# A two-layer decoder trunk on one core: input combinations of the up-projection taken off GpSimd, the last up-projection bank copied ahead of the SiLU, and a down-projection in eight groups

## The chip, the cores and the metric

The kernel runs on one core of a Trainium2 chip. The engines are named as in the profile: PE is TensorE's matrix unit (PEld its weight loads), DVE is VectorE, ACT is ScalarE, POOL is GpSimd, and SP is SyncE, which here only issues DMAs. Each engine works through its own list of instructions in order; an instruction that waits holds up everything behind it on that engine. The metric is the device time of one execution, in microseconds (us), as the median of several runs.

## The reference

Two layers; each has a token mixer (convolution, differential attention, spatial gating) and a channel mixer. Each of the two is wrapped in the same way, `x <- LayerNorm(alpha * x + (1 + gate) * f(x * (1 + scale) + shift))`. The change lies in the channel mixer:

```python
D_MODEL, SEQ, DEPTH = 1024, 1024, 2
FFN_DIM = ((8 * D_MODEL // 3 + 127) // 128) * 128      # 2816: 22 blocks of 128
FFN_KERNEL = 3

def conv_ffn(h, w_up, b_up, conv_w, conv_b, w_down, b_down):
    up = causal_dwconv(h @ w_up + b_up, conv_w, conv_b)
    g, val = jnp.split(up, 2, axis=-1)
    return (jax.nn.silu(g) * val) @ w_down + b_down
```

All data is fp32, batch 1. A product of two fp32 matrices is made of three matmuls on rounded parts: each operand is split into a high part (a cast, on ACT) and the remainder (a subtraction, on DVE or POOL), and high by high, low by high and high by low are added up (`mm3`, lines 128 to 132). Making those two parts is called a split below.

## The kernel before

A layer runs through these stages, with the times of layer 0 and layer 1 in the profiled execution: the mixer until 507 and 1732 us; the last group of its output projection with the LayerNorm of its rows (the boundary) until 530 and 1755; the transposes that turn the rows into inputs of the up-projection until 552 and 1776; the up-projection until 992 and 2206; the down-projection, and in layer 0 the LayerNorm and transposes into layer 1, until 1293 and 2483.

**Input combinations.** The up-projection is done with seven products of half size instead of eight (Strassen's scheme). Its right operands are four quarters of the transposed, modulated input and sums of them, here called B11, B21, B22, T1, T2, T3 and T4. `comb_early` runs once the first half of the rows is normalised, `comb_late` after the second. `comb_in` (L954) transposes four row tiles on PE and writes scale and shift with ACT (L958). `comb_split` (L960) is the split: a cast on ACT (L961) and a subtraction (L962) on the engine that it is given. Before, B22, T3 and T4 were split on POOL, the other four on DVE; the sums were on DVE (L974, L985) and POOL (L988, L989). The left operands (weights) have the same scheme; `up_first` (L1049) makes those of block 0 ahead of time, with four sums on POOL (L1055 to L1064) during the attention. One of its parts, the seventh weight a22, is split at the start of `up_phase` into a page of the tag Rb; it is only read by the last product of block 0, but its cast stands ahead of the copies of `up_phase` on ACT.

**Up-projection.** `up_phase` (L1078) goes over 22 blocks f; PE's, ACT's and DVE's order in it is written by hand (other instructions are put between these by the scheduler). A block is seven products (`product`) of 12 matmuls each, in the order 2, 5, 6, 3, 7, 1 of the next block, 4; products 3 and 1 of block 0 come first. Banks of PSUM are read by copies on ACT. Of the two halves of a block, the gate half `cg` is convolved (`taps`, two L1111 on DVE) and goes through the SiLU (L1193, ACT); the value half is copied from bank `pb` to `cv` (L1133, ACT) in the next turn of the loop, and so is the product of both and its DMA to d_act. For the last block this next turn does no products: it is only the copy, `lin`, `taps`, the multiplication and the DMA.

**Down-projection.** `ffn` (L1226) goes over the 22 blocks in groups of the sizes in L1244. For each block of a group it loads the activation (`load_act`, L1212) and the weight (`load_wdown`, L1218) and splits both. `out_group` (L874) then goes over eight row tiles: the products of the group add up in a pair of banks `og`, and DVE adds the pair to the running sum r (L887); the first group is copied by ACT instead (L885). Two sets of pages hold split operands in turn. After each group, `pump` takes so many steps of a background list: in layer 0 the 47 steps of the modulation of layer 1 (DVE multiply-adds L258 and L260 on DMAs of `wada`) and eight steps of the residual (`residual_in`, L1006: three 128x1024 DVE operations per row tile, L1016 to L1018, on `xr`, with `agab` and `xr` in pages of tag O+"b"); in layer 1 only the residual. The order of the list is fixed in the program, but a scheduler places the instructions on the engines by priority, so the work of later code may come ahead of that of earlier code.

**Boundary of the layers.** After the last group of layer 0, each row tile is normalised (`ln_rows`, L348 to L363; the reciprocal root is on POOL, L138), transposed (L333, PE) and split into the input of layer 1: ACT writes the scaled tile (L340) and its high part (L343), DVE the remainder (L346). Then PE starts the projection `prj` of layer 1.

## Time and profile before

| | us |
|---|---|
| runs, median (lowest to highest) | 2482.52 (2481.01 to 2484.5) |
| profiled execution | 2485.14 |
| its span, first to last instruction | 2483.4 |
| PE busy in it | 2323.6 (94%) |
| DVE busy | 1988.7 (80%) |
| ACT busy | 1049.6 (42%) |
| POOL busy | 402.4 (16%) |
| mean granted TensorE clock | 0.968 |

A row of the timeline reads: start, duration, engine, line, operation, output <- inputs, sizes, how many instructions are drawn together, and in brackets how long the engine was idle before it and which engine's instruction released it. A row of the windows reads: the stretch and its length, then for each engine the busy time and the number of instructions in it, the granted clock, the share of the DMA engines, and GB/s. A row of the waits reads: who waited for whom, us in total, times, longest. A 128x512 matmul at the full clock is drawn 0.39 us long but starts 0.227 us after the one before it.

### The profile page before, as it was taken

The page shows a single profiled execution, that of the slowest core. Times are in us where ns is not written, and L with a number is a line of the kernel's source. Part 1 is how long each engine was busy: PE and PEld are TensorE (multiplying, and loading weights), DVE is VectorE, ACT ScalarE, POOL GpSimd, SP SyncE. Part 2 cuts the span into 40 slices and gives each one's busy share as a digit, 9 for nine tenths or more (in the row PEclk, how much of TensorE's full clock was granted, in tenths as well). Part 3 has the DMA queues.
Part 4 walks back from the last instruction along what each step waited for, and adds up shares of the span by engine and source line. Part 5 has one row for each costly group of instructions (what it writes and reads, how often), then busy time and mean ns, then how long its engine had stood idle before and what let it go on. Part 6 is the DMA issues. An engine that isn't in the chain of part 4 may idle for free.

```text
span 2483.4 us, 28299 instructions
## 1 busy us (share of the span) xinstructions
PE 2323.6 (94%) x10846; PEld 1889.5 (76%) x10846; DVE 1988.7 (80%) x2618; ACT 1049.6 (42%) x1692; POOL 402.4 (16%) x213
## 2 busy tenths in 40 slices
PE   7998999979999999999689999999799999979996
PEld 7786777767888887788578877777588888868885
DVE  7898876788887888778979987657987777787768
ACT  4214754645554554311131157454555545542111
POOL 1144260441000000000020542123500000000003
PEclk9998899989999999999899998999899999989998
DMA  8433352122332334645523254220232222263311
GB/s 295 148 120 130 134 202 103 60 93 94 110 111 94 111 110 157 214 146 176 177 60 115 77 169 160 95 102 26 94 102 77 83 87 86 77 204 127 102 43 68
DMA packets 87673, 294.07 MB, mean 118 GB/s; under 512 B 9265, under 2 KB 18801, under 8 KB 86001
## 3 DMA queue, kind: packets, MB, share of 16 engines
q1 hardware_dynamic: 87536, 292.26, 35.1%
q8 instruction: 85, 1.39, 0.2%
q14 instruction: 52, 0.42, 0.1%
HBM read 228.23 MB, written 64.00 MB: 118 GB/s over the span
## 4 chain that ended last, share of the span: by engine, by line
PE 37%; DVE 9%; issue 3%; ACT 3%; POOL 2%; DMA 1%; SPq 0%; POOLq 0%; DVEq 0%; ACTq 0%
PE og L130 3%; PE og L131 3%; PE og L132 3%; PE upb L1074 3%; PE upb L1076 3%; PE upb L1075 3%; PE sc L733 2%; PE upd L1076 1%; PE upd L1074 1%; PE upd L1075 1%; PE pv L778 1%; DVE r L887 1%; PE of L130 1%; DVE dn L126 1%; PE of L132 1%
## 5 line engine op out<-in xcount | busy, mean ns | idle before, releaser
L130 PE MATMUL og<-dn,dn 128*128 128x512 f32 x704 | 280.3, 398 | 38.6 <-DVE r L887 22.0
L1074 PE MATMUL upb<-comb,uw 128*128 128x512 f32 x704 | 275.6, 392 | 8.6 <-DVE upc L1098 6.7
L1075 PE MATMUL upb<-comb,uw 128*128 128x512 f32 x704 | 275.3, 391 | 2.5 <-DVE comb L962 2.5
L131 PE MATMUL og<-dn,dn 128*128 128x512 f32 x704 | 277.6, 394 | 0.0
L132 PE MATMUL og<-dn,dn 128*128 128x512 f32 x704 | 277.2, 394 | 0.0
L1076 PE MATMUL upb<-comb,uw 128*128 128x512 f32 x704 | 274.9, 391 | 0.0
L138 POOL TENSOR_TENSOR lnrs<-lnrs,mhalf 128x1 f32<-128x1 f32 x32 | 21.2, 666 | 1398.7 <-DVE lnrs L137 1394.1
L1098 DVE TENSOR_TENSOR uw<-wu,uw 128x512 fp32r<-128x512 f32 x210 | 144.0, 686 | 125.2 <-ACT uw L1101 125.2
L1111 DVE SCALAR_TENSOR_TENSOR cv<-upc,pc,cv 128x1023 f32<-128x1023 f32 (+1 forms) x176 | 225.3, 1280 | 2.8
L887 DVE TENSOR_TENSOR r<-og,r 128x1024 f32<-128x1024 f32 x144 | 174.3, 1218 | 64.7 <-PE og L132 63.8
L130 PEld LDWEIGHTS og<-dn,dn 128*128 128x128 f32 x704 | 133.8, 190 | 73.8 <-DVE r L887 27.0
L410 DVE SCALAR_TENSOR_TENSOR convacc<-convy,pc,convacc 128x1023 f32<-128x1023 f32 (+14 forms) x120 | 176.2, 1469 | 2.3
L125 ACT CAST dn<-actr 128x1024 fp32r<-128x1024 f32 x44 | 46.0, 1050 | 310.4 <-PE og L131 146.4
L1074 PEld LDWEIGHTS upb<-comb,uw 128*128 128x128 f32 x704 | 132.7, 188 | 38.5 <-DVE upc L1098 8.4
L1075 PEld LDWEIGHTS upb<-comb,uw 128*128 128x128 f32 x704 | 132.7, 189 | 31.8 <-DVE comb L962 4.2
L1101 ACT CAST uw<-wu 128x512 fp32r<-128x512 f32 x210 | 121.6, 615 | 83.5 <-DVE wu L1098 77.0
L132 PEld LDWEIGHTS og<-dn,dn 128*128 128x128 f32 x704 | 133.8, 190 | 28.2
L131 PEld LDWEIGHTS og<-dn,dn 128*128 128x128 f32 x704 | 134.1, 190 | 26.8
L1076 PEld LDWEIGHTS upb<-comb,uw 128*128 128x128 f32 x704 | 132.7, 189 | 27.5
L1075 PE MATMUL upd<-comb,uw 128*128 128x512 f32 x352 | 138.2, 393 | 3.0 <-DVE comb L962 2.9
L1074 PE MATMUL upd<-comb,uw 128*128 128x512 f32 x352 | 138.0, 392 | 0.0
L1076 PE MATMUL upd<-comb,uw 128*128 128x512 f32 x352 | 137.3, 390 | 0.0
(315 smaller groups left out, 5554.4 us busy)
## 6 DMA issues: line engine op xcount, KB each, us to landing
wada<-in_w_ada SPq DMA_DIRECT2D x96, 512.0 KB, 4.5
wu<-in_w_up_t SPq DMA_DIRECT2D x84, 512.0 KB, 3.6
d_act<-cv SPq DMA_DIRECT2D x44, 512.0 KB, 2.6
actr<-d_act SPq DMA_DIRECT2D x44, 512.0 KB, 4.4
wdn<-in_w_down SPq DMA_DIRECT2D x44, 512.0 KB, 4.5
win<-in_w_fm SPq DMA_DIRECT2D x24, 512.0 KB, 4.2
wtm<-in_w_tm SPq DMA_DIRECT2D x16, 512.0 KB, 3.7
wout<-in_w_out SPq DMA_DIRECT2D x16, 512.0 KB, 6.0
```

What stands on the lines that cost most here:

```text
L130: mm(ps, lh, rh, start=first, stop=False)
L131: mm(ps, lh, rl, start=False, stop=False)
L132: mm(ps, ll, rh, start=False, stop=last)
L410: nc.vector.scalar_tensor_tensor(out=acc[:, d:], in0=y[:, :S - d], scalar=w(30 - d), in1=acc[:, d:], op0=ALU.mult, op1=ALU.add)
L733: nc.tensor.matmul(ps[m][:, c0:c1], q[ms, isl], k[ms, c0:c1], start=n == 0, stop=n == 2 and c1 != w)
L887: nc.vector.tensor_tensor(out=r[t], in0=ps, in1=r[t], op=ALU.add)
L1074: mm(ps, w[:, 0, ks], hi[k], start=k == 0 and not more, stop=False, skip_group_check=True)
L1075: mm(ps, w[:, 0, ks], lo[k], start=False, stop=False, skip_group_check=True)
L1076: mm(ps, w[:, 1, ks], hi[k], start=False, stop=k == 3, skip_group_check=True)
L1098: v.tensor_tensor(out=o, in0=x, in1=y, op=op)
L1101: act.copy(self.up_w[n][:, 0], src)
L1111: v.scalar_tensor_tensor(out=u[:, d:], in0=c[:, :S - d], scalar=self.ffw[:, 2 - d, m:m + 1], in1=u[:, d:], op0=ALU.mult, op1=ALU.add)
```

## The change

Three things are changed in both layers.

1. `comb_early`, `comb_late` and `up_first` issue nothing on POOL any more: all splits and sums of the inputs, and the four sums of the first weights, are on DVE. `comb_early` keeps only the transposes; the splits are put into `comb_late` in the order B22, B11, B21, T1, T2, T3, T4, and the sums are formed in other pages.
2. After the last product of the last block, `up_phase` copies its bank to `cv` at once, ahead of the SiLU in the list of ACT, and the next turn of the loop leaves the copy out.
3. The down-projection has eight groups (2, 3, 3, 3, 3, 3, 2, 3) instead of nine (2, 3, 3, 3, 3, 2, 2, 1, 3). The activations of the first group get two pages of tag O+"b" of their own, and the two sets of pages change places. `pump` takes 3n steps after a group of n instead of 3n + 2, and after the first group none in layer 1.

```diff
     def comb_early(self, r, H, sc, sh):
         nc = self.nc
         H["f3"] = self.parts("tmp", 2, F32)
-        f22 = self.parts("tmp", 2, F32)
+        H["f22"] = self.parts("tmp", 2, F32)
         for k in range(4):
-            self.comb_in(r, 1, k + 4, sc, sh, f22[k])
-            self.comb_split(H["B22"], k, f22[k], nc.gpsimd)
+            self.comb_in(r, 1, k + 4, sc, sh, H["f22"][k])
         for k in range(4):
-            f12, f3 = H["f12"][k], H["f3"][k]
-            self.comb_in(r, 1, k, sc, sh, f12)
-            nc.vector.tensor_tensor(out=f3, in0=f22[k], in1=f12, op=ALU.subtract)
-            self.comb_split(H["T3"], k, f3, nc.gpsimd)
+            self.comb_in(r, 1, k, sc, sh, H["f12"][k])
...
         f = self.parts("Rb", 2, F32) + self.parts("Rb", 2, F32)
-        f1, f2 = H["f12"], H["f3"]
-        for q in range(8):
+        f1, f2, f22 = H["f12"], H["f3"], H["f22"]
+
+        def tt(o, x, y, op):
+            nc.vector.tensor_tensor(out=o, in0=x, in1=y, op=op)
+        for k in range(4):
+            self.comb_split(H["B22"], k, f22[k], nc.vector)
+        for q in range(4):
             self.comb_in(r, 0, q, sc, sh, f[q])
-            self.comb_split(H["B11" if q < 4 else "B21"], q % 4, f[q], nc.vector)
+        for q in range(4):
+            self.comb_split(H["B11"], q, f[q], nc.vector)
+        for q in range(4, 8):
+            self.comb_in(r, 0, q, sc, sh, f[q])
+        for q in range(4, 8):
+            self.comb_split(H["B21"], q - 4, f[q], nc.vector)
         for k in range(4):
-            nc.vector.tensor_tensor(out=f1[k], in0=f1[k], in1=f[k], op=ALU.subtract)
+            tt(f2[k], f22[k], f1[k], ALU.subtract)
+            tt(f1[k], f1[k], f[k], ALU.subtract)
             self.comb_split(H["T1"], k, f1[k], nc.vector)
         for k in range(4):
-            nc.gpsimd.tensor_tensor(out=f2[k], in0=f2[k], in1=f[k], op=ALU.add)
-            nc.gpsimd.tensor_tensor(out=f[4 + k], in0=f[4 + k], in1=f2[k], op=ALU.subtract)
-            self.comb_split(H["T2"], k, f2[k], nc.vector)
+            tt(f[k], f2[k], f[k], ALU.add)
+            tt(f[4 + k], f[4 + k], f[k], ALU.subtract)
+            self.comb_split(H["T2"], k, f[k], nc.vector)
         for k in range(4):
-            self.comb_split(H["T4"], k, f[4 + k], nc.gpsimd)
+            self.comb_split(H["T3"], k, f2[k], nc.vector)
+        for k in range(4):
+            self.comb_split(H["T4"], k, f[4 + k], nc.vector)
...
-        tt = nc.gpsimd.tensor_tensor
+        tt = nc.vector.tensor_tensor
...
             if f:
-                act.copy(cv[:, 0:512], pb)
+                if run:
+                    act.copy(cv[:, 0:512], pb)
...
             pb = b
+            if not nxt:
+                act.copy(cv[:, 0:512], pb)
...
         yb, yc = pages(A + "b", 4), pages(A + "c", 4)
-        sets = [(ya[:6], yc + ya[6:]), (xa[:6], xa[6:] + yb)]
+        xb = []
+        for _ in range(2):
+            t = self.page(O + "b", "dn", F32R, (P, 2, 1024))
+            xb += [t[:, i] for i in range(2)]
+        sets = [(xa[:6], xa[6:] + yb), (ya[:6], yc + ya[6:])]
...
-        sizes = (2, 3, 3, 3, 3, 2, 2, 1, 3)
+        sizes = (2, 3, 3, 3, 3, 3, 2, 3)
...
-            acts, wts = (ya[:4], xc) if j == 0 else sets[j % 2]
+            acts, wts = (xb, xc) if j == 0 else sets[j % 2]
...
-                self.pump(2)
+                    self.pump(2)
...
-                self.pump(3 * n + 2 if l + 1 < L else 2)
+                self.pump(3 * n if l + 1 < L else 2)
```

Lines behind the change have other numbers in the changed kernel: L974, L985, L988 and L989 become L979, L1098 becomes L1107, L1133 becomes L1143 (and the new copy L1200), L1193 becomes L1205.

How the lists of instructions change is shown at three places. The first is DVE's list of layer 0 at the end of the combinations, before. `comb` are the combinations and their parts, `uw_849_4593` is the low part of weight a22, made from a page of `wuv` by its split, and `wus` and L1098 are the first sums of block 1.

```order
L962 TENSOR_TENSOR comb_758_4174<-comb_820_4460,comb_756_4172 128x512 x2
L126 TENSOR_TENSOR uw_849_4593<-wuv_740_4138,uw_849_4593 128x512
L962 TENSOR_TENSOR comb_759_4175<-comb_821_4461,comb_757_4173 128x512 x2
L962 TENSOR_TENSOR comb_750_4166<-comb_764_4180,comb_760_4176 128x512 x2
L962 TENSOR_TENSOR comb_750_4166<-comb_765_4181,comb_761_4177 128x512 x2
L962 TENSOR_TENSOR comb_751_4167<-comb_790_4290,comb_762_4178 128x512 x2
L962 TENSOR_TENSOR comb_751_4167<-comb_791_4291,comb_763_4179 128x512 x2
L1098 TENSOR_TENSOR wus_836_4580<-wu_847_4591 128x512
```

The same end of the combinations on DVE in the changed kernel:

```order
L962 TENSOR_TENSOR comb_750_4166<-comb_765_4181,comb_761_4177 128x512
L979 TENSOR_TENSOR comb_821_4441<-comb_821_4441,comb_819_4439 128x512
L962 TENSOR_TENSOR comb_750_4166<-comb_765_4181,comb_761_4177 128x512
L962 TENSOR_TENSOR comb_751_4167<-comb_818_4438,comb_762_4178 128x512 x2
L962 TENSOR_TENSOR comb_751_4167<-comb_819_4439,comb_763_4179 128x512 x2
L962 TENSOR_TENSOR comb_768_4184<-comb_820_4440,comb_766_4182 128x512 x2
L962 TENSOR_TENSOR comb_769_4185<-comb_821_4441,comb_767_4183 128x512 x2
L126 TENSOR_TENSOR uw_849_4593<-wuv_740_4138,uw_849_4593 128x512
L1107 TENSOR_TENSOR wus_836_4580<-wu_847_4591 128x512
```

The splits of T4 (`comb_768`, `comb_769`) and the sums L979 are new on this engine, and the split of weight a22 has gone from among the combinations to behind the last of them.

The second place is ACT's list at the end of the up-projection of layer 1, before. `upe_13216<-upb` is the last copy of block 21's other bank, `cv_13222<-cv_13222` is the SiLU, `upc_13220<-upb_15830` the copy of the last bank; the casts are splits of activations (`actr`) and weights (`wdn`) of the first groups of the down-projection.

```order
L1166 COPY upe_13216<-upb_15830 128x512
L125 CAST dn_15980<-actr_16143 128x1024
L125 CAST dn_15981<-wdn_16155 128x1024
L1107 ACTIVATE cv_13222<-upc_13219,ffcc_13200,pc_91 128x1024
L125 CAST dn_15982<-wdn_16160 128x1024
L125 CAST dn_15984<-wdn_16165 128x1024
L125 CAST dn_15980<-actr_16147 128x1024
L125 CAST dn_15981<-actr_16151 128x1024
L1193 ACTIVATE cv_13222<-cv_13222 128x1024
L1133 COPY upc_13220<-upb_15830 128x512
```

The same in the changed kernel:

```order
L1176 COPY upe_13202<-upb_15816 128x512
L125 CAST dn_15954<-actr_16118 128x1024
L125 CAST dn_15974<-wdn_16135 128x1024
L1116 ACTIVATE cv_13208<-upc_13205,ffcc_13186,pc_91 128x1024
L125 CAST dn_15956<-actr_16122 128x1024
L125 CAST dn_15958<-actr_16126 128x1024
L1200 COPY upc_13206<-upb_15816 128x512
L125 CAST dn_15960<-wdn_16140 128x1024
L1205 ACTIVATE cv_13208<-cv_13208 128x1024
```

The copy stands ahead of the SiLU and of one weight cast, and still behind three casts of activations. On SP's list the loads of `agab` and `xr`, which stood around the first of these activation loads, have gone behind the DMA of the last product to d_act and many later loads.

The third place is PE's list at the end of layer 0's last group, before. `og` is the group's pair of banks, `tr` are the transposes into layer 1.

```order
L131 MATMUL og_9155<-dn_7414,dn_7395 128x512
L333 MATMUL tr_9014<-ident,r_7439 128x128
L333 MATMUL tr_9014<-ident,r_7440 128x128
L333 MATMUL tr_9014<-ident,r_7441 128x128
L333 MATMUL tr_9014<-ident,r_7442 128x128
L333 MATMUL tr_9023<-ident,r_7439 128x128
L333 MATMUL tr_9023<-ident,r_7440 128x128
L333 MATMUL tr_9023<-ident,r_7441 128x128
L333 MATMUL tr_9023<-ident,r_7442 128x128
L132 MATMUL og_9155<-dn_7413,dn_7396 128x512
```

PE's list at the end of the last group in the changed kernel; `modp` and `gatet` are the last modulation of layer 1:

```order
L132 MATMUL og_9141<-dn_7399,dn_7398 128x512
L269 MATMUL modp_8625<-ones,macc_7560 128x1 x8
L286 MATMUL gatet_8638<-ident,gatec_8421 16x128
L333 MATMUL tr_8982<-ident,r_7441 128x128
L333 MATMUL tr_8982<-ident,r_7442 128x128
L333 MATMUL tr_8982<-ident,r_7443 128x128
L333 MATMUL tr_8982<-ident,r_7444 128x128
L333 MATMUL tr_8991<-ident,r_7441 128x128
```

All 64 transposes now stand behind the last matmul of the group; before, 16 of them stood among its matmuls.

## The prediction

> **What bounds the kernel now.** The page first: PE is busy 94% of the span, so the whole prize is the rest, some 160 us, wherever PE waits; the other engines count only where PE waits for them.
>
> ```profile
> span 2483.4 us, 28299 instructions
> PE 2323.6 (94%) x10846; PEld 1889.5 (76%) x10846; DVE 1988.7 (80%) x2618; ACT 1049.6 (42%) x1692; POOL 402.4 (16%) x213
> L887 DVE TENSOR_TENSOR r<-og,r 128x1024 f32<-128x1024 f32 x144 | 174.3, 1218 | 64.7 <-PE og L132 63.8
> ```
>
> Next the windows of the four stretches that the change touches: the combinations of layer 1, the end of its up-projection, and the second half of the down-projection of layer 0.
>
> ```profile
> 1753.00:1776.00 23.00, 14.00 (x65) 10.06 (x64) 21.00 (x25) 17.74 (x30) 18.14 (x14) 0.66 0.40 147
> 1776.00:1800.00 24.00, 18.13 (x70) 12.51 (x69) 24.00 (x23) 13.63 (x25) 15.98 (x10) 0.97 0.08 24
> ...
> 2206.00:2221.00 15.00, 2.84 (x13) 2.02 (x11) 14.40 (x14) 8.16 (x9) 0.00 (x0) 0.67 0.68 218
> ```
>
> ```profile
> 1144.00:1240.00 96.00, 75.76 (x315) 59.33 (x315) 94.00 (x89) 13.88 (x14) 0.00 (x0) 0.89 0.60 195
> ```
>
> DVE (third figure) is full from 1776 to 1800, with POOL (fifth) at work beside it, and again for 94.00 of 96 us from 1144 to 1240, while PE (first) has 6 and 20 us to spare. From 2206 to 2221 PE does almost nothing. The waits of PE say for whom:
>
> ```profile
> PE upb L1074 <- DVE upc L1098: 5.0, 1, 5.0
> PE og L130 <- DVE r L887: 2.5, 2, 1.6
> PE og L130 <- DVE r L887: 17.7, 6, 9.9
> PE og L130 <- ACT upc L1133: 12.2, 1, 12.2
> PE og L130 <- DVE r L887: 1.9, 3, 0.6
> ```
>
> They are, in order: layer 0 at the end of the up-projection (986), in its groups (1144 to 1190, 1190 to 1240), layer 1 at the end of the up-projection (2221) and in its groups (2380 to 2430). Beside these PE waits in the combinations of both layers. Everything below is about these waits.
>
> **Combinations on DVE alone (both layers).** Of a layer's 44 operations, 24 were on DVE and 20 on POOL.
>
> ```profile
> L962 DVE TENSOR_TENSOR comb<-comb,comb x32: 675/1754/1784, 547.9 to 1796.2; 128x512 fp32r<-128x512 f32 x32
> L962 POOL TENSOR_TENSOR comb<-comb,comb x24: 1266/1710/1762, 532.8 to 1794.0; 128x512 fp32r<-128x512 f32 x24
> ...
> 1779.06 2.48 DVE L962 TENSOR_TENSOR comb<-comb,comb 128x512 fp32r<-128x512 f32 x4
> ...
> 1783.16 13.75 DVE L962 TENSOR_TENSOR comb<-comb,comb 128x512 fp32r<-128x512 f32 x10
> 1796.84 0.68 DVE L1098 TENSOR_TENSOR wus<-wu 128x512 f32<-128x512 f32 x1
> ```
>
> The same DVE operation takes 1754 ns in the median and 675 at best. The four at 1779.06 (POOL between two operations, which start at 1775.16 and, after a pause, at 1781.07) take 2.48 us, 0.62 each; the ten at 1783.16, with POOL busy, take 1.375 each. So POOL's operations (1710 ns in the median) cost DVE about as much as they save it: 44 on DVE alone are 44 x 0.62 = 27.3 us, against the 36.7 us from the first sum in the second half of the rows (1760.14) to 1796.84, when DVE is through.
>
> ```profile
> 1760.14 1.76 DVE L974 TENSOR_TENSOR comb<-comb,comb 128x512 f32<-128x512 f32 x1 [0.76 <-ACT comb L958]
> ...
> 1781.07 3.32 POOL L989 TENSOR_TENSOR comb<-comb,comb 128x512 f32<-128x512 f32 x2 [2.49 <-issue]
> ...
> 1775.16 3.42 POOL L988 TENSOR_TENSOR comb<-comb,comb 128x512 f32<-128x512 f32 x2
> ```
>
> 27.3 from 1760.14 gives 1787.4, 9.4 us earlier. What PE makes of it: its products 3, 1, 2, 5, 6, 7, 1' and 4 of block 0 run from 1776.44 to 1807.76, in 31.3 us, of which 8 x 12 x 0.227 = 21.8 are matmuls.
>
> ```profile
> 1776.44 0.78 PE L1074 MATMUL upd<-comb,uw 128*128 128x512 f32 x1
> ...
> 1784.99 0.50 PE L1075 MATMUL upa<-comb,uw 128*128 128x512 f32 x1 [0.75 <-DVE comb L962]
> ...
> 1807.76 0.39 PE L1074 MATMUL upa<-comb,uw 128*128 128x512 f32 x1
> ```
>
> Walked through the new lists with these durations, the first product starts at 1774.1, 2.3 earlier, and products 3, 1, 2 and 5 then run without a pause to 1785.0. But the split of weight a22 now stands behind the last split of T4 (1787.4): its cast on ACT ends at 1788.1, the copy of product 1's bank behind it at 1788.6, and product 6, which adds to that bank, waits 3.7 us. The next block starts at 1800.5 instead of 1807.76: 7.2 us gained, of 11.9 that there would be without that wait. `up_first` gives some back: its first sum waits on POOL for a page that the attention frees.
>
> ```profile
> 1718.14 1.29 POOL L1056 TENSOR_TENSOR wus<-wuv 128x512 f32<-128x512 f32 x1 [9.53 <-PE pv L778]
> ```
>
> On DVE this wait holds up what stands behind it, one addition of the output projection and through it PE, by about 1.1 us. So 6.1 a layer, 12.2 for both.
>
> Does the new wait slow the clock? Two rows of PE, with the matmuls behind them:
>
> ```profile
> 986.82 0.80 PE L1074 MATMUL upb<-comb,uw 128*128 128x512 f32 x1 [5.03 <-DVE upc L1098]
> 987.41 0.63 PE L1075 MATMUL upb<-comb,uw 128*128 128x512 f32 x1
> ...
> 992.11 0.54 PE L130 MATMUL og<-dn,dn 128*128 128x512 f32 x1
> ...
> 1002.62 0.50 PE L130 MATMUL og<-dn,dn 128*128 128x512 f32 x1 [1.89 <-ACT r L885]
> 1002.96 0.39 PE L131 MATMUL og<-dn,dn 128*128 128x512 f32 x1
> ```
>
> Behind 5.03 us of idleness the twelve matmuls to 992.11 take 5.3 us instead of 2.7; behind 1.89 none is slow. 3.7 lies between, and costs 0 or 2.6 a layer; I take 0 and make the other a rival. [...]
>
> **Last copy (layer 1).** PE waits 12.2 us until 2221.04 for the copy, and ACT's rows say why that is late: the casts ahead of it wait for their DMAs, and the SiLU for DVE.
>
> ```profile
> 2205.52 1.05 ACT L125 CAST dn<-actr 128x1024 fp32r<-128x1024 f32 x1 [8.01 <-DMA actr<-d_act]
> ...
> 2215.64 1.04 ACT L125 CAST dn<-actr 128x1024 fp32r<-128x1024 f32 x1 [3.12 <-DMA actr<-d_act]
> 2219.46 1.06 ACT L1193 ACTIVATE cv<-cv 128x1024 f32<-128x1024 f32 x1 [2.77 <-DVE cv L1098]
> 2220.42 0.57 ACT L1133 COPY upc<-upb 128x512 f32<-128x512 f32 x1
> ```
>
> The copy leaves the SiLU's shadow (2.77 + 1.06) but still stands behind the cast of 2215.64, which waits for its DMA. If that lands as before, the copy starts at 2216.7, ends at 2217.2, and the gain is 3.8. It should land earlier: `agab` and `xr`, four loads, are no longer on SP around the activation loads (SP's list), and the DMA share here is 0.68. With all waits on DMA gone, the gain would be the 12.2, less 2.2 because DVE's new list splits one activation and more ahead of the last subtraction before product 4. I take the copy at about 2213, 7 us gained, nearer the middle of 3.8 and 10.
>
> **Layer 0, last copy and eight groups.** Product 4 waited 5.03 us because its ACT cast waited for the same kind of DMA:
>
> ```profile
> 982.73 1.04 ACT L125 CAST dn<-actr 128x1024 fp32r<-128x1024 f32 x1 [5.75 <-DMA actr<-d_act]
> ```
>
> Without `agab` and `xr` ahead of that load (0.9 us of issue on SP and their transfers) I put product 4 at about 984.2, 2.6 earlier; a wait of 2.4 should leave the clock up, which the slow twelve make worth up to 2.6 more. I take 4. A group less is eight additions L887 less, 8 x 1.218 = 9.7 us of DVE where DVE is full. The pump's smaller steps move residual additions, three 1.2 us operations per tile, towards the last two groups, and all transposes into layer 1 come behind the last matmul. Their price, from the end before:
>
> ```profile
> 1275.66 1.23 DVE L887 TENSOR_TENSOR r<-og,r 128x1024 f32<-128x1024 f32 x1
> ...
> 1288.52 1.97 PE L333 MATMUL tr<-ident,r 128*128 128x128 f32 x8 [1.35 <-ACT hf L340]
> 1290.89 1.97 PE L333 MATMUL tr<-ident,r 128*128 128x128 f32 x8 [0.40 <-ACT hf L340]
> 1292.51 0.60 PE L130 MATMUL prj<-h,wh 128*128 128x512 f32 x1
> ```
>
> The projection starts 16.9 us after the last L887. Eight transposes are two banks and take 2.37 us (1288.52 to 1290.89), at ACT's pace; 16 banks are 19.0, and with the wait at their start 21.5: 4.6 lost. So 4 + 9.7 - 4.6 = 9.1 by DVE's work. Walking the new lists with the durations puts the last L887 at about 1257, 18.7 earlier, for PE's 20.2 us of waits go too, and the projection at 1278.5: 14.0. I take 11.5, between the two.
>
> **Eight groups (layer 1).** Here DVE is not full; of the waits only 1.9 us hang on L887. I take 2 (0 to 3). The tail behind the last group is as before.
>
> **Sum.** 12.2 + 7 + 11.5 + 2 = 32.7 from the profiled execution's 2485.14 gives 2452.4; the median of the runs shown is 2.6 below that execution, so 2450 is the forecast, 1.3% faster.
>
> **The rivals.**
> - *Half the gain.* DMAs land as before (copy 3.8), product 6's wait halves the clock in both layers (12.2 - 5.2 = 7), layer 0 gives 5, layer 1's groups nothing: 16, so 2467. For it: casts of activations still stand ahead of the copy. Against: the transfers ahead of them are fewer.
> - *Layer 0's end takes its part back.* Residual additions bunch up behind the last groups, transposes wait for the last LayerNorm, and the 11.5 are gone: 2462. For it: DVE is full there (94.00 of 96). Against: eight additions less are work less.
> - *The clock alone:* product 6's wait slows the matmuls behind it, 5.2 us: 2455.
> - *Slower: DVE's 1754 ns are not POOL's doing* but belong to an operation with a rounded output behind one on ACT. Then 44 operations take 44 x 1.375 = 60.5 us instead of 36.7, 23.8 a layer, and with the other 20.5 us gained it is 2482.5 - 20.5 + 47.6 = 2510. It decides from 0.83 us an operation (36.7 / 44) that the combinations cost time, and from 1.07 that the whole does. Against: the 2.48 us of four.
> - *Nothing but the combinations moves* because ACT and DVE wait for the same DMAs: 12.2 alone, 2470.
>
> **How the numbers follow.** The forecast has 0.45, the clock alone 0.15, half the gain 0.15, layer 0's end 0.1, nothing but the combinations 0.05, slower 0.05; 0.05 is left for more (11.9 - 1.1 a layer, 10 and 14: 2437). The range goes from 2436 to 2471: it leaves out the slower case and the tails of the others. Of half the gain, 0.04 is with combinations at 0.75 us instead of 0.62, 44 x 0.13 = 5.7 a layer: 2478, within 0.2% of no change. 0.2%, 5 us, is about what a measurement of this kernel can tell from no change. Faster 0.91, same 0.04, slower 0.05.
>
> **What would show it.** Right: DVE's L962 at 0.6 to 0.7 us throughout, from the first matmul of block 0 to that of block 1 about 26 us instead of 31.3, product 6 waiting 3 to 4 us for ACT's copy; `og` of layer 1 waiting some 5 us for the copy instead of 12.2; L887 x128; the waits for L887 in layer 0 below 5 us, and 64 transposes in one run behind its last group, at about 1.2 us a bank. Wrong: L962 still above 1 us on DVE, PE waiting for L887 at the end of layer 0 as before, or the copy at 2216 or later.

## The result, and the profile after

| | before | after |
|---|---|---|
| runs, median (lowest to highest), us | 2482.24 (2481.01 to 2484.5) | 2438.93 (2437.79 to 2442.12) |
| profiled execution, us | 2485.14 | 2437.79 |

The changed kernel takes 0.9826 of the time before (95% interval 0.9812 to 0.984): 43.3 us less, where 32.5 were forecast (2450, from the median of 2482.52 that was known then). The two profiled executions differ by 47.4, because that of before lies 2.9 above its median and that of after 1.1 below its own. The page of after:

```profile
span 2436.1 us, 28260 instructions
PE 2308.1 (95%) x10846; PEld 1886.4 (77%) x10846; DVE 1956.1 (80%) x2650; ACT 1049.9 (43%) x1692; POOL 328.9 (13%) x165
L887 DVE TENSOR_TENSOR r<-og,r 128x1024 f32<-128x1024 f32 x128 | 155.7, 1218 | 59.0 <-PE og L132 58.4
```

POOL has lost 73.5 us of work and DVE, which took it over, has not become busier: it went from 1988.7 to 1956.1. Only 18.6 of that are the sixteen L887 that are gone.

To see where the time went, the span is cut at the first matmul of each stage in PE's timeline: `og` of the mixer, block 1 of the up-projection, `og` of the down-projection, `prj` of layer 1, and the same again. The columns before and after are one profiled execution each. The first row moves between 505.1 and 507.9 over all kernels of this document, mostly without any edit that touches it, so a difference of 2 us in a mixer is not to be read; the boundaries repeat within 0.1 in most kernels.

| stage | before | after | difference |
|---|---|---|---|
| to the first og (mixer, layer 0) | 507.7 | 507.1 | -0.7 |
| boundary, og to block 1, layer 0 | 75.7 | 67.0 | -8.7 |
| up-projection, layer 0 | 408.7 | 404.4 | -4.3 |
| down-projection to prj, layer 0 | 300.4 | 291.0 | -9.4 |
| mixer, layer 1 | 439.6 | 438.8 | -0.7 |
| boundary, layer 1 | 75.7 | 67.0 | -8.7 |
| up-projection, layer 1 | 398.2 | 400.2 | +2.0 |
| down-projection to the end, layer 1 | 277.4 | 260.8 | -16.7 |

The combinations. All splits are on DVE, and each takes what the fastest one took before; the shortest and the longest are 12 ns apart:

```profile
L962 DVE TENSOR_TENSOR comb<-comb,comb x56: 677/681/689, 532.6 to 1763.1; 128x512 fp32r<-128x512 f32 x56
```

Windows of layer 1's boundary after; as before, DVE is full, but PE (first figure) has 21.48 of 24 us instead of 18.13 of 24:

```profile
1727.00:1750.00 23.00, 14.87 (x78) 10.49 (x77) 22.56 (x41) 18.44 (x31) 4.06 (x3) 0.85 0.44 160
1750.00:1774.00 24.00, 21.48 (x93) 16.82 (x92) 23.93 (x39) 16.50 (x29) 0.00 (x0) 1.00 0.11 35
```

The end of layer 1's up-projection. The waits of PE from 2150 to 2260 are small, and none is for the copy:

```profile
PE upb L1083 <- DVE upc L1107: 2.8, 1, 2.8
PE og L130 <- ACT r L885: 1.3, 1, 1.3
```

ACT's timeline there: the casts of activations still wait for their DMAs (3.21 and 1.26), and the copy comes 3.1 us after the first og (2175.35); before, it came 14.5 us after it (2220.42 and 2205.96).

```profile
2175.20 1.05 ACT L125 CAST dn<-actr 128x1024 fp32r<-128x1024 f32 x1 [3.21 <-DMA actr<-d_act]
2177.51 1.05 ACT L125 CAST dn<-actr 128x1024 fp32r<-128x1024 f32 x1 [1.26 <-DMA actr<-d_act]
2178.47 0.58 ACT L1200 COPY upc<-upb 128x512 f32<-128x512 f32 x1
2178.95 1.06 ACT L125 CAST dn<-wdn 128x1024 fp32r<-128x1024 f32 x1
2179.90 1.06 ACT L1205 ACTIVATE cv<-cv 128x1024 f32<-128x1024 f32 x1
```

The end of layer 0. The waits for L887 (20.2 us before) are gone from PE's groups, and one wait of 22 us stands in their place, at the transpose of the last modulation row, ahead of all transposes into layer 1:

```profile
1227.44 1.84 PE L269 MATMUL modp<-ones,macc 128*128 128x1 f32 x16
1251.32 0.38 PE L286 MATMUL gatet<-ident,gatec 128*16 128x128 f32 x1 [22.04 <-DVE gatec L283]
...
1263.88 5.87 PE L333 MATMUL tr<-ident,r 128*128 128x128 f32 x20 [0.26 <-ACT hf L340]
```

DVE's timeline in that time; the last L887 starts 21.7 us after PE has left the group for the modulation (1227.44), between residual additions (L1025 to L1027), LayerNorm (L352, L363) and modulation:

```profile
1241.94 1.17 DVE L887 TENSOR_TENSOR r<-og,r 128x1024 f32<-128x1024 f32 x1
1243.03 2.34 DVE L277 TENSOR_SCALAR gatec<-gatec 128x8 f32<-128x8 f32 x1
1245.28 1.21 DVE L1027 TENSOR_TENSOR r<-r,xr 128x1024 f32<-128x1024 f32 x1
...
1249.18 1.21 DVE L887 TENSOR_TENSOR r<-og,r 128x1024 f32<-128x1024 f32 x1
...
1251.16 0.11 DVE L283 SCALAR_TENSOR_TENSOR gatec<-pc,gatec 128x8 f32<-128x8 f32 x1
```

So three things were to be found out: which part of the change took the 16.7 us at the end of layer 1, for which 9 were forecast; why layer 0 gained what it did with DVE still behind; and whether the parts add up.

### The profile page after: what moved, and what is told of

It reads as the page before. It is cut to its first block, busy times and chain, and to the rows that moved or that the text cites. A ratio compares the mean times of both kernels' runs of the same rounds, so it can differ in the third digit from the quotient of the medians.

```text
span 2436.1 us, 28260 instructions
## 1 busy us (share of the span) xinstructions
PE 2308.1 (95%) x10846; PEld 1886.4 (77%) x10846; DVE 1956.1 (80%) x2650; ACT 1049.9 (43%) x1692; POOL 328.9 (13%) x165
## 4 chain that ended last, share of the span: by engine, by line
PE 67%; DVE 17%; issue 6%; ACT 4%; DMA 3%; POOL 2%; SPq 0%; POOLq 0%; DVEq 0%; ACTq 0%
PE upb L1083 6%; PE upb L1084 6%; PE upb L1085 6%; PE og L130 5%; PE og L131 5%; PE og L132 5%; PE sc L733 3%; PE upd L1084 3%; PE upd L1085 3%; PE upd L1083 3%; DVE convacc L410 2%; PE pv L778 2%; PE of L130 2%; PE of L132 2%; PE of L131 2%
## 5 line engine op out<-in xcount | busy, mean ns | idle before, releaser
L130 PE MATMUL og<-dn,dn 128*128 128x512 f32 x704 | 275.3, 391 | 2.6 <-ACT r L885 2.1
L131 PE MATMUL og<-dn,dn 128*128 128x512 f32 x704 | 274.5, 390 | 0.0
L132 PE MATMUL og<-dn,dn 128*128 128x512 f32 x704 | 274.3, 390 | 0.0
L1107 DVE TENSOR_TENSOR uw<-wu,uw 128x512 fp32r<-128x512 f32 x210 | 144.1, 686 | 125.3 <-ACT uw L1110 125.3
L887 DVE TENSOR_TENSOR r<-og,r 128x1024 f32<-128x1024 f32 x128 | 155.7, 1218 | 59.0 <-PE og L132 58.4
L130 PEld LDWEIGHTS og<-dn,dn 128*128 128x128 f32 x704 | 132.2, 188 | 31.5 <-ACT r L885 3.4
L132 PEld LDWEIGHTS og<-dn,dn 128*128 128x128 f32 x704 | 132.2, 188 | 27.4
L131 PEld LDWEIGHTS og<-dn,dn 128*128 128x128 f32 x704 | 132.2, 188 | 26.8
```

The lines of the kernel that those rows point to most:

```text
L130: mm(ps, lh, rh, start=first, stop=False)
L131: mm(ps, lh, rl, start=False, stop=False)
L132: mm(ps, ll, rh, start=False, stop=last)
L887: nc.vector.tensor_tensor(out=r[t], in0=ps, in1=r[t], op=ALU.add)
L1107: v.tensor_tensor(out=o, in0=x, in1=y, op=op)
```

## The experiments

All times are medians beside runs of the kernel before on the same chip (2482.51 for the four runs from part 1 alone to after without part 2, 2482.75 for the two with pump 3n + 2 or the row moved alone, eight sizes alone and after without part 1, 2481.47 for the rest); ratios have 95% intervals. The stages of all twelve, cut as above from one profiled execution each:

| kernel | median | boundary (each layer) | layer 0, og to prj | mixer, layer 1 | layer 1, og to end |
|---|---|---|---|---|---|
| before | 2482.2 | 75.7 | 300.4 | 439.6 | 277.4 |
| after | 2438.9 | 67.0 | 291.0 | 438.8 | 260.8 |
| part 1 alone | 2472.7 | 67.0 | 302.7 | 445.0 | 276.3 |
| part 2 alone | 2462.5 | 75.7 | 295.7 | 439.3 | 263.1 |
| part 3 alone | 2459.0 | 75.6 | 293.5 | 437.6 | 263.6 |
| after without part 2 | 2446.6 | 67.0 | 296.8 | 438.2 | 261.5 |
| after without part 1 | 2455.1 | 76.0 | 289.1 | 437.0 | 263.1 |
| eight sizes alone | 2469.3 | 75.7 | 285.8 | 441.7 | 274.7 |
| after, pump 3n + 2 | 2434.2 | 67.0 | 283.4 | 443.6 | 259.6 |
| after, last row moved | 2434.1 | 67.0 | 277.3 | 442.4 | 260.9 |
| own pages alone | 2472.7 | 75.6 | 302.2 | 437.3 | 270.2 |
| after, first sums on POOL | 2436.2 | 67.0 | 288.9 | 439.5 | 259.9 |
| last row moved and 3n + 2 | 2421.1 | 67.0 | 270.1 | 439.0 | 260.3 |
| after, pump 3n + 3 | 2431.9 | 67.0 | 283.6 | 440.9 | 260.1 |

### The parts one by one

A second theory had come from the listing of the program: the bank of PSUM that the last product of layer 1 uses is number 5 before and 6 after, and the second row tile of the down-projection writes banks 4 and 5.

**Part 1 alone:** the first hunks of the diff (`comb_early`, `comb_late`, and in `up_first` the line below), on the kernel before.

```diff
-        tt = nc.gpsimd.tensor_tensor
+        tt = nc.vector.tensor_tensor
```

> Part 1 alone (combinations and first weights off GpSimd). Theory A, the prices of the prediction: 6.1 us a layer and nothing at the end of the up-projection, so 2482 - 12 = 2470, with the wait of the down-projection of layer 1 for the copy of the last bank still at about 12 us. Theory B, the bank: the program gives the last product of layer 1 another bank (6 instead of 5) as soon as part 1 is in, and bank 6 is written by none of the first row tiles of the down-projection; then the 12.2 us wait is gone with part 1 alone though the copy is not moved, and with 9 us a layer from the combinations the time is 2482 - 18 - 14 = 2450.

Measured: 2472.67, 0.9962 (0.9948 to 0.9977). Near A's number, for other reasons, and not B's. The boundaries are 8.7 shorter each, as in the full change, but 2.3 us are lost in layer 0's down-projection and 5.4 in the mixer of layer 1. The bank is 6, and the wait for the copy has gone; yet the stretch to the end is as long as before, since PE, two tiles further on, waits for ACT all the same. Its waits from 2150 to 2270:

```profile
PE og L130 <- ACT r L885: 11.6, 2, 10.0
PE upb L1083 <- DVE upc L1107: 0.9, 1, 0.9
```

So the bank decides which tile waits, as theory B had it, but not the time: how long is set by ACT's list, in which the first copies L885 stand behind the same casts, SiLU and copy. Theory B's gain of 14 us at that place is refuted.

**Part 2 alone:**

```diff
             if f:
-                act.copy(cv[:, 0:512], pb)
+                if run:
+                    act.copy(cv[:, 0:512], pb)
...
             pb = b
+            if not nxt:
+                act.copy(cv[:, 0:512], pb)
```

> Part 2 alone (the last copy moved ahead of the SiLU). In its list of ACT the copy stands ahead of both casts of activations that waited for DMAs, and the bank is 5, as before. Both theories: the second row tile of layer 1 starts at about 2211 instead of 2221, a gain of 10, 2472; in layer 0 nothing. A third, that the wait is set by something else than the copy: 2482.

Measured: 2462.53, 0.9922 (0.9907 to 0.9937), a gain of 20 and not 10. The first two rows of ACT's timeline at the end of layer 1 below are the mechanism as expected: the copy no longer waits for the activations, though `agab` and `xr` are where they were. What was not expected stands behind them: the three copies L885 come ahead of the SiLU as well, so the later tiles do not wait either.

```profile
2199.89 0.58 ACT L1191 COPY upc<-upb 128x512 f32<-128x512 f32 x1
2200.72 1.05 ACT L125 CAST dn<-actr 128x1024 fp32r<-128x1024 f32 x1 [0.25 <-DMA actr<-d_act]
2203.90 1.06 ACT L125 CAST dn<-actr 128x1024 fp32r<-128x1024 f32 x1 [2.13 <-DMA actr<-d_act]
2204.86 2.84 ACT L885 COPY r<-og 128x1024 f32<-128x1024 f32 x3
2208.91 1.06 ACT L1196 ACTIVATE cv<-cv 128x1024 f32<-128x1024 f32 x1 [1.21 <-DVE cv L1098]
```

Of the 277.4 us 14.4 are gone: nearly the whole 12.2 (0.9 is left) and the slow matmuls behind it. The same in layer 0 gives 4.7 us, where I had expected nothing: there PE waited for L885 (1.89 and 1.31 us), and its waits for L887 are 1.5 shorter too.

**Part 3 alone:** the hunks of `ffn`.

> Part 3 alone (eight groups, own pages for the first activations, smaller pump steps). Theory A: 11.5 in layer 0, 2 in layer 1's groups, and 3.8 to 7 at the end of its up-projection because agab and xr no longer stand ahead of the activation loads: 2482 - 19 = 2463. Theory B: layer 0 gives 4.3 + 9.4 as between the two kernels, but the bank of layer 1 is 5 as before and the copy stands behind three casts of activations and the SiLU, so that wait stays above 8: 2482 - 13.7 - 4 = 2464; what tells them apart is that wait, 5 to 8 us by A, over 8 by B.

Measured: 2458.98, 0.9905 (0.9891 to 0.992). The wait for the copy is 2.6 us with bank 5 and with the copy behind casts and SiLU, below what either theory gave it:

```profile
PE upb L1074 <- DVE upc L1098: 2.8, 1, 2.8
PE og L130 <- ACT upc L1133: 2.6, 1, 2.6
```

The stretch to the end is 13.9 shorter. So part 2 and part 3 each remove nearly all of the same wait, by different means, and alone they give 9.8 + 20.0 + 23.5 = 53.3 us with part 1, while together it is 43.3. Why the casts wait less is seen on SP. Before, the next activation loads were issued 6.0 us after the store of the product to d_act; the row of the timeline of before:

```profile
2201.88 0.32 SPq L1159 DMA_DIRECT2D d_act<-cv  x1
2207.85 1.76 SPq L1214 DMA_DIRECT2D actr<-d_act  x2
```

and after, where no `agab` and `xr` are in flight, 1.7 us:

```profile
2170.14 0.33 SPq L1169 DMA_DIRECT2D d_act<-cv  x1
2171.87 1.39 SPq L1226 DMA_DIRECT2D actr<-d_act  x2
```

In part 1 alone, part 2 alone and eight sizes alone, which have the old pages, it is 5.2, 4.7 and 6.3; in part 3 alone and in own pages alone 1.7. So it goes with the pages of the first activations and not with the sizes. That these loads wait for the page which the store reads is argued from the code, not shown.

**After without part 2:** the copy of the changed kernel put back.

> The changed kernel without part 2: the copy of the last bank is back behind the SiLU. Theory A: part 2 gave the larger part of the 7 us in layer 1, so 2439 + 4 = 2443 at least, and PE waits for the copy. Theory B: the bank is 6, no row tile of layer 1 waits for it, and in layer 0 the third tile writes the bank and may wait 0 to 2 us: 2439 to 2441.

Measured: 2446.55, 0.9857 (0.9842 to 0.9872): 7.6 us more than the changed kernel, above the 4 of theory A, and in another place. Layer 1's stretch to the end loses 0.7. Its up-projection loses 1.6 by slow matmuls behind PE's wait of 2.76 us at product 4; kernels that have part 2 show these as well, so they are not part 2's, and some 6 us are left for it. Layer 0's stretch loses 5.8, by one wait of PE for L885 and the slow matmuls behind it:

```profile
984.88 0.50 PE L130 MATMUL og<-dn,dn 128*128 128x512 f32 x1 [0.48 <-ACT upc L1142]
994.00 0.80 PE L130 MATMUL og<-dn,dn 128*128 128x512 f32 x1 [6.07 <-ACT r L885]
```

**After without part 1:** combinations and first weights back on POOL.

> The changed kernel with part 1 undone (combinations and first weights back on GpSimd). Theory A, the parts add up where they lie apart: from the start of the down-projection's boundary to block 1 it was 75.7 us in each layer with GpSimd and 67.0 without, whatever else is in the kernel, so 2439 + 2 x 8.7 = 2456. Theory B, the gain of part 1 is partly given back later, as in the run of part 1 alone (10 us gained of 17.4): 2439 + 10 = 2449.

Measured: 2455.14, 0.9889 (0.9875 to 0.9904). Theory A: the boundaries are 8.7 and 9.3 longer, and the sum is 16.2. Part 1 adds to the others, though alone it gave 9.8.

### What the eight groups and the pump do in layer 0

**Eight sizes alone**, on the kernel before:

```diff
-        sizes = (2, 3, 3, 3, 3, 2, 2, 1, 3)
+        sizes = (2, 3, 3, 3, 3, 3, 2, 3)
```

> Only the list of sizes changed in the kernel before: eight groups, with the old pages for the first activations and the old pump of 3n + 2. Theory A, the additions: eight L887 less in layer 0 where DVE is full, 9.7 us less at most what the order of the transposes takes, so layer 0's down-projection shortens by 5 to 10 us, and nothing at the end of layer 1's up-projection (12.2 us wait for the copy as before): 2475. Theory B, the pages: the gain of part 3 is the activation loads that no longer stand behind agab and xr; then the sizes alone give under 3 us: 2480.

Measured: 2469.32, 0.9948 (0.9933 to 0.9963). More than A gave: layer 0's down-projection is 14.6 us shorter. DVE has eight additions less (9.7 us), and PE's waits for L887 fall from 20.2 to 2.9, with one of 4.8 for the last modulation in their place. Layer 1 has a 12.6 us wait for the copy as before. This one line did more in layer 0 than all of part 3 (6.9), so something in part 3 takes back what it gives.

**After, with the old pump:**

```diff
-                self.pump(3 * n if l + 1 < L else 2)
+                self.pump(3 * n + 2 if l + 1 < L else 2)
```

> The changed kernel with the pump at 3n + 2 steps a group again (eight groups, all else as changed): the residual additions of layer 0 come earlier. Theory A, DVE's work in the last two groups bounds the end of layer 0 (DVE full from 1190 to 1255, PE idle 22 us before the last modulation's transpose): earlier additions use DVE's idle time of 1040 to 1140, and the projection of layer 1 starts 3 to 8 us earlier, 2434. Theory B, PE's order bounds it (all transposes behind that one): no change, 2439. Against both: DMAs of the modulation crowded out, slower, 2443.

Measured: 2434.23, 0.981 (0.9795 to 0.9824). Theory A: the stretch to prj is 7.6 shorter than with 3n, and the wait for the last modulation falls from 22.0 to 8.0:

```profile
PE gatet L286 <- DVE lnrs L137: 8.0, 1, 8.0
PE og L130 <- DVE r L887: 4.6, 3, 2.4
```

But the mixer of layer 1 takes 4.8 more: PE waits 3.8 us there for DVE's L767 instead of 0.2, and some matmuls at its end run at half the clock (below). In the median 4.7 are left, of which some 2 lie in layer 0's mixer, which the edit does not touch. The smaller pump was the part that took back. A step more, 3n + 3:

> The changed kernel with the pump at 3n + 3. The stretch from layer 0's first og to the projection is 291.0 us with 3n and 283.4 with 3n + 2. Theory A (residual additions moved into DVE's idle time): about 283 or a little less. Theory B (a balance, DMAs of the modulation are now late): above 284. PE's list of layer 1's mixer is another one again; if that list and not the earlier start sets the 438.8 against 443.6 us of that stage, then it can come out at 438 and the time at 2429; if an earlier end of layer 0 is always given back there, 443 and 2434.

Measured: 2431.87, 0.9796 (0.9781 to 0.981). The stretch is 283.6: as with 3n + 2, so this step brings nothing more there; the mixer comes out at 440.9, between the two numbers expected, so the question about it stays open.

**The last modulation row moved** from layer 0's down-projection into layer 1's up-projection:

```diff
-        wa = [self.page("Ra", "wada") for _ in range(2 if l == 0 else 0)]
+        wa = [self.page("Ra", "wada") for _ in range(2)]
...
+        self.mod_cfg = (None, None)
+        self.mod_tile = wa + [self.page("rows", "macc")]
+        mods = self.mods(l, (5,))
         if l == 0:
-            self.mod_cfg = (None, None)
-            self.mod_tile = wa + [self.page("rows", "macc")]
-            later = self.mods(1, (1, 0, 2, 3, 4, 5))
-            mods = chain(self.mods(0, (5,)), later)
+            later = self.mods(1, (1, 0, 2, 3, 4))
+            mods = chain(mods, later)
...
-            if 0 < f < NF - 2:
+            if (0 if l == 0 else 3) < f < NF - 2:
```

> The changed kernel with the last modulation row of layer 1 (eight DVE multiply-adds of 1.28 us and its transpose) taken out of layer 0's down-projection and put into layer 1's up-projection, where DVE is busy 78%. Theory A (DVE bounds the end of layer 0): 10 us less on DVE there and no gatet ahead of the transposes, so the projection starts 6 to 10 us earlier, 2431, with layer 1's up-projection unchanged. Theory B (the transposes at ACT's pace bound it): the transposes start when the rows are ready, 1.2 us a bank, gain under 3: 2437.

Measured: 2434.12, 0.9811 (0.9794 to 0.9827). Theory A for the stretch: 13.7 us shorter, more than the 10.2 of DVE's work, since PE no longer stands behind `gatet`. Two places give back: the mixer 3.6, and layer 1's up-projection 3.6, where PE's wait of 2.75 us at product 4 is now followed by nine matmuls at half the clock, 0.43 us apart (some 1.8 of the 3.6), and in the run of after by none, 0.23 apart. Theory A's 2431 left both out.

**Both:** the row moved (begun at block 8), and 3n + 2.

> The run with the last modulation row in layer 1's up-projection (begun at block 8) and the pump at 3n + 2 as well. Theory A (DVE's work at the end of layer 0 is still the bound): the residual additions come earlier too, and the stretch from layer 0's first og to the projection falls below 277 to 270 to 274. Theory B (with that row gone the transposes at ACT's pace bound it): 277 as without. The attention of layer 1 has a third list of PE here; it took 437 to 439 us from the projection to og in some lists and 442 to 445 in others. So 2424 to 2431 by A, 2428 to 2434 by B.

Measured: 2421.05, 0.9758 (0.9743 to 0.9772): the fastest, 17.9 us below the changed kernel. Theory A: 270.1 us, another 7.2 less; DVE's work still bounds the end of layer 0, as the two steps that took work away from there show. The transposes of the first half stand among the group's matmuls again, and PE waits only for the last LayerNorm and for ACT:

```profile
PE tr L333 <- ACT hf L340: 4.9, 6, 1.3
PE tr L333 <- DVE r L363: 4.6, 1, 4.6
PE og L130 <- DVE r L887: 0.2, 1, 0.2
```

### Two single costs

**Own pages alone**, on the kernel before:

```diff
+        xb = []
+        for _ in range(2):
+            t = self.page(O + "b", "dn", F32R, (P, 2, 1024))
+            xb += [t[:, i] for i in range(2)]
         sets = [(ya[:6], yc + ya[6:]), (xa[:6], xa[6:] + yb)]
...
-            acts, wts = (ya[:4], xc) if j == 0 else sets[j % 2]
+            acts, wts = (xb, xc) if j == 0 else sets[j % 2]
```

> The kernel before, with only the two pages of their own for the first activations (nine groups, old pump, old order of the two sets, copy behind the SiLU): agab and xr, which use pages of the same tag, are loaded after the activations. Theory A (the loads ahead of the activation loads held ACT's casts, and these the copy): layer 1's stretch from the first og to the end falls from 277.4 to about 264, and layer 0's up-projection by 4; 2482 - 13 - 4 + 2 = 2467. Theory B (eight groups made part 3's gain there): 277 as before, 2480.

Measured: 2472.73, 0.9962 (0.9948 to 0.9975). Partly A: layer 0's up-projection is 5.6 shorter, and the wait for the copy falls to 2.7; but the stretch to the end falls by 7.2 and not by 13, with a new wait of 2.8 for L887. So the pages take most of the wait for the copy, but only half of what part 3 gains at this place. Which of the other edits of part 3 (the order of the two sets, the sizes) brings the rest is open.

**First sums back on POOL**, in the changed kernel:

```diff
-        tt = nc.vector.tensor_tensor
+        tt = nc.gpsimd.tensor_tensor
```

> The changed kernel with the four sums of the first weights back on GpSimd. The prediction charged 1.1 us a layer to them on DVE (they wait in DVE's list for a page of the attention): by that 2439 - 2 = 2437. Rival: the mixers are as long in both kernels (507.7 and 507.1; 439.6 and 438.8), so they cost nothing: 2439. If the sums on GpSimd slow DVE's additions beside them: 2441.

Measured: 2436.19, 0.9815 (0.9798 to 0.9831), 2.7 below the changed kernel, whose ratio (0.9826) the interval still holds, so the totals do not decide; 2441 lies outside it. The boundaries are the same 67.0. The traces decide: at the end of the output projection PE waits 1.84 us for L862 with the sums on DVE, the first row (after), and 0.78 with them on POOL, the second row (this run).

```profile
495.81 0.50 PE L130 MATMUL of<-woh,ybh 128*128 128x512 f32 x1 [1.84 <-DVE r L862]
493.47 0.51 PE L130 MATMUL of<-woh,ybh 128*128 128x512 f32 x1 [0.78 <-DVE r L862]
```

That is the 1.1 us of the prediction. But two waits behind it become shorter with the sums on DVE (one of 0.64 is gone, one of 0.78 falls to 0.34). From PE's wait for L862 ahead of these (0.73) to the first og it is 24.5 to 24.6 us with the sums on DVE, in layer 0 of all seven such kernels, and 23.9 to 24.0 with them on POOL, in both layers of all seven: these sums cost 0.6 us a layer, neither 1.1 nor nothing.

In layer 1 of three of the seven (part 1 alone, 3n + 2, 3n + 3) it is 25.7 to 27.0, since there the longer wait is followed by matmuls at half the clock. Rows and windows of part 1 alone; the figure ahead of the last two is the granted clock, full until the wait and half behind it:

```profile
1715.81 0.66 PE L130 MATMUL of<-woh,ybh 128*128 128x512 f32 x1 [1.83 <-DVE r L862]
1716.26 0.63 PE L131 MATMUL of<-wol,ybh 128*128 128x512 f32 x1
1712.00:1716.00 4.00, 2.17 (x11) 1.48 (x11) 3.76 (x8) 1.31 (x4) 0.00 (x0) 1.00 0.00 0
1716.00:1722.00 6.00, 5.22 (x12) 3.53 (x12) 1.73 (x4) 0.00 (x0) 1.01 (x1) 0.50 0.00 0
```

## Why the prediction was right, and where its sizes were off

**What bounds the kernel.** Right: 45.9 of the 47.4 us between the two profiled executions lie in the stretches that it named, and DVE's count of L887 fell to 128.

**Combinations on DVE alone: right, 8.7 a layer instead of 6.1.** Splits are drawn 0.68 us long and start 0.60 apart with POOL out of the way, and DVE is through 9.3 us earlier counted from the first og of the boundary (55.4 us after it instead of 64.8; 9.4 were worked out). From the first matmul of block 0 to that of block 1 it is 24.7 us in layer 0 and 25.3 in layer 1 (31.3 before, about 26 forecast). Part 1 also changes the order of the splits; no run has the new order with the work still on POOL, but the price of an operation accounts for DVE's 9.3 by itself. The slower rival, that 1754 ns belong to the operation, is refuted. Two terms were mis-sized, and a sum slipped: from the copy at 1788.6 four products of 2.7 us end at 1799.5 and not at 1800.5, so the walk gives 8.2 and not 7.2. Product 6 was to wait 3.7 us for the copy behind the cast of weight a22, and waited 1.0:

```profile
1762.05 0.50 PE L1083 MATMUL upb<-comb,uw 128*128 128x512 f32 x1 [1.00 <-ACT upe L1127]
```

The cast began at 1760.16 while the splits of T4 ran until 1763.66: DVE released it after the third of the last nine splits, so it does not need the last of all. And `up_first` costs 0.6 us a layer, not 1.1: the longer wait came as worked out, and PE won part of it back behind.

**The clock.** The rival did not come to its test in the changed kernel, since the wait was 1.0. Part 1 alone has a wait of nearly that length, at the start of layer 0's down-projection.

```profile
994.12 0.80 PE L130 MATMUL og<-dn,dn 128*128 128x512 f32 x1 [3.73 <-ACT r L885]
994.72 0.63 PE L131 MATMUL og<-dn,dn 128*128 128x512 f32 x1
```

Here the matmuls start 0.43 us apart instead of 0.227, at half the clock, so my choice of "0" was badly founded. Nor does 1.89 us bound it from below: behind a wait of 1.83 the clock was half in part 1 alone, and behind one of 3.59 at another place (last row moved and 3n + 2, at 166.80) it was not. What a wait of 3.7 us would have done at product 6 stays open.

**Last copy, layer 1: the right wait, half the size.** The prediction had the copy at about 8 us earlier, with a rest of some 5 us; it came 11.3 earlier, counted from the first og, and no tile waited for it. 7 us were forecast there and 2 for the groups; measured are 16.7 less the 2.0 that product 4 is later (2.2 were forecast), 14.7. The groups are right: their 1.9 us of waits for L887 are gone. The term that was mis-sized is the 7, in two ways. It was put between the worth of the copy's place in ACT's list and that of the DMAs ahead of it, as if one alone left a rest; the runs show either edit as enough, part 3 alone with 13.9 and part 2 alone with 14.4, and with part 3 in place moving the copy is worth 0.7 in layer 1. And its bound of 10 left out the matmuls at half the clock behind the 12.20 us wait (eight of them, 1.8 us; in the run of before those behind the first start 0.43 us apart). Of part 3's 13.9, own pages alone give 7.2; what gives the rest is open. The bank adds a little: with bank 5 and both (after without part 1) PE waits 2.1 us for the copy, with 6 none.

**Layer 0: 13.7 instead of 11.5.** Product 4's place gave 4.3 (4 forecast). It waited 1.35 us for DVE, and the matmuls behind start 0.23 us apart, at the full clock. That a wait of 2.4 would leave the clock up was an estimate between the rows at 1.89 and 5.03: behind one of 2.48 in the mixer the matmuls were at half the clock in the run of after (at 81.24, granted 0.50) and not in that of 3n + 3 (at 78.75). The walk through the lists had said 14.0 for both, and the average with the sum of DVE's work was the worse number. The walk had DVE right: the last L887 came 17.1 us earlier counted from block 1 (18.7 worked out), and the projection 20.2 behind it (21.5). It had PE wrong: "PE's 20.2 us of waits go too" did not come about, since the wait of 22.0 at the last modulation stands in their place; the waits for L887 are below 5 us only by name. The end came earlier because DVE had less to do, not because PE waited less. Both missed that two edits work against each other: the sizes take 14.6 us, the smaller pump gives 7.6 back, and part 2, which was to give nothing in layer 0, holds 5.8.

**The rivals.** The result lies 1.9 us from the case of more (2437), which was given 0.05, and 2.9 from the lower end of the range: the direction is right, three of the four terms came out larger than forecast, and that the sum stayed inside the range is partly luck. Half the gain and layer 0's end did not come about; layer 0's end is a true mechanism, though: the wait of 22 us is it, and with DVE's work moved away it is worth 20.9 us (291.0 to 270.1).

## What to carry to other kernels

A wait names the instruction that came last, not its cause: here a copy on ACT was late because of the list ahead of it, which ran in order (it started at 2220.42 behind casts that had waited 8.01 and 3.12 us, and at 2199.89 in its new place in part 2 alone), and either part 3, which among other things takes away the loads that delayed that list, or the copy's new place in it took nearly the whole wait, so the two gains do not add. When work is taken off an engine that is full near the end of a stage, look at where its background work falls: the smaller pump costs 7.6 us, half of the 14.6 that one group less gains by itself. And compare stages, not only totals: part 1 gained 17.4 us where it was meant to and lost 7.7 elsewhere when alone.

## What the runs showed that I had not expected

- The mixer of layer 1, of which the edits touch only the sums of the first weights, takes 437.0 to 445.0 us over these kernels. PE's list in it differs: part 1 alone and the run with the last row moved have the same one and took 445.0 and 442.4; before, part 3 alone, after without part 1, own pages alone and first sums on POOL share another and took 437.0 to 439.6. In the ones above 441 PE waits up to 3.3 us for DVE's L767 in the attention, and part 1 alone and 3n + 2 have the half clock at the end of the mixer as well, as 3n + 3 (440.9) has. The list goes with the wait for L767; that it alone is the cause was not tried.
- PE's waits of 3.73 (part 1 alone), 4.43 (own pages alone), 5.03 (before) and 6.07 us (after without part 2) in the products were each followed by slow matmuls, which start 0.43 us apart instead of 0.227 in the first three; shorter ones went either way. Nine kernels have a wait of 2.75 or 2.76 us at product 4 of layer 1's last block. In three (after, part 3 alone, after without part 1) no slow matmul follows and the up-projection takes 400.2 us; in six some eight follow, and it takes 401.4 to 401.8, or 403.8 with the row moved. So some 1.5 us of the changed kernel's profiled time is luck. No run shows what decides between the two outcomes.
- The store to d_act and the loads behind it: issued 1.7 us apart without other loads of 512 KB just ahead (after, part 3 alone, own pages alone), 4.7 to 6.3 with four of them (`agab` and `xr`) issued before the store (before, part 1 alone, part 2 alone, eight sizes alone).
